# Ten projections' low weight parts: ACT negates the high part, a transfer issued by POOL adds the weight

## Chip, cores and metric

The kernel runs on one core of one Trainium2 chip. The metric is device time in microseconds. The engines are named as in the profile: PE (matrix products), PEld (its weight loads), DVE, ACT, POOL and SP (which issues most transfers).

## What is computed

One layer of a hybrid block on 512 tokens of width 1024. The change touches the first projection, `z = n1 @ w_in`, whose columns feed three consumers:

```python
n1 = rmsnorm(h, g_mix[i])
z = n1 @ w_in[i]
y_ssm = s5_mixer(z[..., OFF_SSM:OFF_Q], ...)                 # 512 columns
y_nsa = nsa_mixer(z[..., OFF_Q:OFF_KV], z[..., OFF_KV:OFF_NSA_GATE], z[..., OFF_NSA_GATE:OFF_MERGE], ...)
merge = jax.nn.sigmoid(z[..., OFF_MERGE:].astype(jnp.float32))
```

After it come the mix of both branches, an output product, a convolutional feed-forward part and a gated embedding.

## The kernel before

**Split products.** A product of two fp32 matrices is made of three products of a type with fewer bits. Each operand is split in a high part (a copy into that type, by ACT, L76) and a low part (operand minus high part, by DVE or POOL, L55); `mm3` (L83 to L85) multiplies high by high, high by low and low by high, all into one accumulator. The low-by-low product is left out.

**Projections.** `proj` computes 128 columns of `z` for all 512 tokens. It loads a 128x1024 tile of `w_in` (`wr`, 512 KB, `wraw`, L183), splits it into `wh` and `wl` (`wload`), and then runs `mm3` for each of KD = 8 slices: 24 products of 128x512. There are twelve calls: four for the SSM input (`un` copies, L590), four for the queries (`QT`), two for the compressed keys and values (`FL`) and two for the keys (`KK`). The first two get weights that were split earlier (`uw`); the other ten call `wload` with DVE as the engine for the low part. `wr` has three buffers, `wh` and `wl` two each, and the accumulators `pj` of the projections two (`acc`). A `wl` buffer is written again only when the projection two back has read it.

**Around them.** From the sixth projection on, PE does small products of the state-space part between them: `wbps` (transposes, L640), `wps` (L648), `tps` (L668), `yps` (L702, L705), four times over (`ssm_quarter`). Their operands come from all engines: `tab` (a table of rotations) and `x` (powers times an output matrix) from POOL, `z` and the scans from DVE, `Z`, `CX` and `WB` (copies) from ACT. The last of the ten projections is followed by the compression, the gates and attention.

**Order.** Each engine takes its instructions in one fixed order. In the first part (to the V columns) it is written by hand; in the part with the projections a planner sets it when the kernel is built, by its own table of costs. An instruction that waits holds up all behind it on its engine.

Of the kernel before, what the change touches and what calls it, by code (L numbers as in the profile page):

```python
# [9 lines left out]
F32 = mybir.dt.float32  # L10
F32R = mybir.dt.float32r
I32 = mybir.dt.int32
AF = mybir.ActivationFunctionType
# [3 lines left out]
MUL, ADD, SUB = ALU.mult, ALU.add, ALU.subtract  # L17

P = 128
# [3 lines left out]
KD = D // P  # L23
# [11 lines left out]
INW = 3864  # L35
# [10 lines left out]
def hybrid_kernel(ctx: ExitStack, tc: tile.TileContext, A, out):  # L46
    nc = tc.nc
    V, G, S, PE = nc.vector, nc.gpsimd, nc.scalar, nc.tensor

    def dr(name, off, ap):  # L50
        t = A[name]
        return bass.AP(tensor=t.tensor, offset=t.offset + off, ap=ap)
# [22 lines left out]
    def copy(o, a):  # L75
        S.activation(o, a, AF.Copy)  # L76

    def split(hi, lo, src, e=V):
        copy(hi, src)
        tt(lo, src, hi, SUB, e)  # L80

    def mm3(ps, lh, ll, rh, rl, start, stop):
        PE.matmul(ps, lh, rh, start=start, stop=False)  # L83
        PE.matmul(ps, lh, rl, start=False, stop=False)  # L84
        PE.matmul(ps, ll, rh, start=False, stop=stop)  # L85

    def pool(name, bufs=1, side=None, space=None):
        kw = {"name": name, "bufs": bufs, "reuse_waits": "tile"}
        if side:
            kw["side"] = side  # L90
        if space is not None:
            kw["space"] = space
        return tc.tile_pool(**kw)
# [3 lines left out]
    pw = ctx.enter_context(pool("weights", 2))  # L97
# [3 lines left out]
    def bank(tag, name):  # L101
        return psp.tile([P, 512], F32, tag=tag, name=name, bufs=BANKS[tag])

    def slot(p, tag, shape, dt, name):
        return p.tile(shape, dt, tag=tag, name=name, bufs=1)
# [69 lines left out]
    def either():  # L175
        turn[0] ^= 1
        return ("acc", "o")[turn[0]]

    def wraw(name, ld, row0, c0, kt, c, raw=None):
        if raw is None:  # L180
            raw = pw.tile([P, kt * c], F32, name="wr", tag="wr", bufs=3)
            raw = raw.rearrange("p (k c) -> p k c", k=kt)
        nc.sync.dma_start(raw, dr(name, row0 * ld + c0, [[ld, P], [P * ld, kt], [1, c]]))  # L183
        return raw

    def wload(name, ld, row0, c0, kt, c, e=V, keep=None, raw=None):
        if raw is None:
            raw = wraw(name, ld, row0, c0, kt, c)
        if keep is None:
            hi = pw.tile([P, kt * c], F32R, name="wh", tag="wh").rearrange("p (k c) -> p k c", k=kt)  # L190
            lo = pw.tile([P, kt * c], F32R, name="wl", tag="wl").rearrange("p (k c) -> p k c", k=kt)
        else:
            hi, lo = keep
        split(hi, lo, raw, e)
        return hi, lo

    def proj(c0, e=V, w=None):
        hi, lo = w or wload("w_in", INW, 0, c0, KD, P, e)
        ps = bank("acc", "pj")
        for k in range(KD):  # L200
            mm3(ps, hi[:, k], lo[:, k], n1h[:, k], n1l[:, k], k == 0, k == KD - 1)
        return ps

    n1h = slot(pn, "nh", [P, KD, T], F32R, "n1h")
    n1l = slot(pn, "nl", [P, KD, T], F32R, "n1l")
# [347 lines left out]
    for lv in range(5):  # L553
        n = 1 << lv
# [32 lines left out]
    for ct in range(4):  # L587
        un = pw.tile([P, L, NCH], F32, name="un", tag="mg")
        copy(un, proj(ct * P, w=uw[ct] if ct < 2 else None).rearrange("p (c j) -> p j c", j=L))
        nc.sync.dma_start(ud[ct], un)  # L590
        for j in range(L):
            n = L - 1 - j
            nc.sync.dma_start(Uc[32 * n:32 * n + 32, 4 * ct:4 * ct + 4], ud[ct, :, j].rearrange("(a c) k -> c a k", c=32))
# [135 lines left out]
    def compress_in(i):  # L729
        ps = proj(OFF_KV + i * P)  # L730
        for g in range(2):
            for j in range(2):
                x = ps[64 * g:64 * g + 64, j:j + 1]
                (V.tensor_copy if g else copy)(
                    FL[64 * j:64 * j + 64, i, :, g, 0:NCMP - 1],
                    bass.AP(tensor=x.tensor, offset=x.offset, ap=[x.ap[0], [2, 16], [16, NCMP - 1]]))

    def queries(i):
        ps = proj(OFF_Q + i * P)
        split(QT[:, i, 0], QT[:, i, 1], ps)  # L740
# [123 lines left out]
    for hc in range(2):  # L864
        hi, lo = wload("ssm_w_glu", SSMW, 0, hc * 256, 4, 256, V)
        if hc == 0:
            compressed_t(NQ - 1, scs[NQ - 1])
        for cc in range(2):
            c = 2 * hc + cc
            ps = bank(either(), "glu")  # L870
# [160 lines left out]
    for d2 in range(4):  # L1031
        hi, lo = wload("w_br_nsa", D, 0, d2 * 256, 4, 256, V)
        for dd in range(2):
            dt_ = 2 * d2 + dd
            ps = bank(either(), "br")
            for k in range(4):
                c = dd * P
# [22 lines left out]
    ps = bank("s", "cvps")  # L1060
# [8 lines left out]
    for qp in range(2):  # L1069
        for hf, qt in ((0, 0), (0, 1), (1, 0), (1, 1)) if qp == 0 else ((0, 2), (1, 2), (0, 3), (1, 3)):  # L1070
            cs = slice(hf * 512, hf * 512 + 512)
            qs_ = slice(qt * P, (qt + 1) * P)
            ps = bank(either(), "wo")
# [164 lines left out]
    with tc.manual_schedule(engines={mybir.EngineType.PE}):  # L1238
# [17 lines left out]
        for c in range(NR):  # L1256
            for i in range(2):
                hi, lo = wload("w_down", D, 2 * c * P, i * 512, 2, 512)
# [61 lines left out]
        for n, c in enumerate(range(NR, NP)):  # L1320
            h = hid[c]
            hi, lo = wload(None, 0, 0, 0, 2, 512, raw=b1[c].parts())
# [217 lines left out]
```

## Time and profile before

| | |
|---|---|
| time, median of 3 runs | 823.71 us (823.54 to 823.76) |
| the profiled execution | 823.98 us |
| its span in the trace | 822.2 us |
| PE busy | 803.7 us, 98% |
| DVE, ACT, POOL busy | 526.8, 395.4, 256.3 us |
| granted PE clock, mean | 0.997 of full speed |

The profile is one execution. Its own time is 1.8 us longer than its span, and 0.27 us above the median of the runs. Idle time of an engine costs something only where the engine is the one that sets the end. Matmuls overlap: one of 128x512 shows 0.39 us, while the next starts 0.23 us after it.

### The profile page before, as it was taken

How to read it: one execution, taken by the hardware profiler on the slowest of the kernel's cores; microseconds unless marked ns; L12 is line 12 of the kernel's file. 1: busy time of each engine (PE TensorE's matmuls, PEld its weight loads, DVE VectorE, ACT ScalarE, POOL GpSimd, SP SyncE). 2: the span in 40 equal slices, each digit the busy share in tenths (PEclk: the TensorE clock that was granted, in tenths of full speed). 3: DMA queues.
4: the chain of work that ended last, by engine and by line, in shares of the span. 5: the costliest groups of instructions: out<-in, count | busy, mean ns of one | idle time of the engine just before them, and what ended most of it. 6: DMA issues, size and time to landing. Idle time of an engine off the chain costs nothing. (4 is left out here: it accounts for less than half of the span.)

```text
span 822.2 us, 12258 instructions
## 1 busy us (share of the span) xinstructions
PE 803.7 (98%) x4523; PEld 674.4 (82%) x4523; DVE 526.8 (64%) x1102; ACT 395.4 (48%) x734; POOL 256.3 (31%) x316
## 2 busy tenths in 40 slices
PE   6999999999999999999999999999999999999995
PEld 5877889888888888888898888888888888888885
DVE  6899988757677631685444444554445759998743
ACT  4437553546777743434443444444434433675422
POOL 6595111126555633231033223333333100000411
PEclk9999999999999999999999999999999999999998
DMA  9663322423334323343052333323332453332011
GB/s 242 165 167 103 92 65 65 104 77 103 78 78 121 111 56 103 126 134 99 1 154 78 103 102 103 102 85 96 103 91 89 125 170 141 103 128 78 26 52 51
DMA packets 112001, 83.66 MB, mean 102 GB/s; under 512 B 9665, under 2 KB 97477, under 8 KB 111942
## 3 DMA queue, kind: packets, MB, share of 16 engines
q1 hardware_dynamic: 111262, 81.82, 34.5%
q10 hardware_dynamic: 680, 1.07, 0.3%
q8 instruction: 35, 0.57, 0.3%
q14 instruction: 24, 0.20, 0.1%
HBM read 75.54 MB, written 3.15 MB: 96 GB/s over the span
## 5 line engine op out<-in xcount | busy, mean ns | idle before, releaser
L55 POOL TENSOR_TENSOR wl<-wr,wh 128x1024 fp32r<-128x1024 f32 x39 | 94.0, 2409 | 247.8 <-ACT wh L76 229.9
L76 ACT ACTIVATE wh<-wr 128x1024 fp32r<-128x1024 f32 x88 | 93.1, 1059 | 93.7 <-issue 27.7
L55 DVE TENSOR_TENSOR wl<-wr,wh 128x1024 fp32r<-128x1024 f32 x49 | 62.7, 1280 | 54.0 <-ACT wh L76 54.0
L83 PE MATMUL pj<-n1h,wh 128*128 128x512 f32 x224 | 91.0, 406 | 0.3 <-ACT un L76 0.3
L85 PE MATMUL pj<-n1h,wl 128*128 128x512 f32 x224 | 88.1, 394 | 0.4 <-DVE wl L55 0.4
L84 PE MATMUL pj<-n1l,wh 128*128 128x512 f32 x224 | 88.0, 393 | 0.0
L64 DVE SCALAR_TENSOR_TENSOR cv<-ub,cvp,cv 128x511 f32<-128x511 f32 (+1 forms) x44 | 32.9, 748 | 66.2 <-ACT cv L1202 65.4
L84 PE MATMUL ua<-n2l,wh 128*128 128x512 f32 (+1 forms) x176 | 66.9, 380 | 0.2 <-DVE n2l L64 0.2
L83 PE MATMUL ua<-n2h,wh 128*128 128x512 f32 (+1 forms) x176 | 66.9, 380 | 0.0
L84 PE MATMUL ub<-n2l,wh 128*128 128x512 f32 (+1 forms) x176 | 66.8, 379 | 0.0
L85 PE MATMUL ua<-n2h,wl 128*128 128x512 f32 (+1 forms) x176 | 66.8, 379 | 0.0
L85 PE MATMUL ub<-n2h,wl 128*128 128x512 f32 (+1 forms) x176 | 66.8, 379 | 0.0
L83 PE MATMUL ub<-n2h,wh 128*128 128x512 f32 (+1 forms) x176 | 66.8, 379 | 0.0
L85 PEld LDWEIGHTS pj<-n1h,wl 128*128 128x128 f32 x224 | 42.1, 188 | 10.2 <-DVE wl L55 1.1
L61 POOL TENSOR_SCALAR pr<-pr,su,gates 128x512 f32<-128x512 f32 (+1 forms) x64 | 39.2, 623 | 31.1 <-DVE su L913 28.5
L83 PEld LDWEIGHTS pj<-n1h,wh 128*128 128x128 f32 x224 | 42.1, 188 | 8.0 <-ACT un L76 0.6
L84 PEld LDWEIGHTS pj<-n1l,wh 128*128 128x128 f32 x224 | 42.2, 188 | 7.7 <-issue 0.6
L55 POOL TENSOR_TENSOR wg1l<-wr,wg1h 128x1024 fp32r<-128x1024 f32 x2 | 7.0, 3506 | 111.1 <-ACT wg1h L76 111.1
L55 DVE TENSOR_TENSOR pl<-ptp,ph 128x128 fp32r<-128x128 f32 (+1 forms) x64 | 31.2, 488 | 15.2 <-ACT ph L76 14.9
L912 ACT ACTIVATE pr<-pr,nb 128x512 f32<-128x512 f32 (+1 forms) x64 | 35.6, 557 | 7.2 <-DVE nb L910 7.2
L76 ACT ACTIVATE ph<-ptp 128x128 fp32r<-128x128 f32 (+1 forms) x64 | 27.7, 433 | 22.9 <-PE ptp L921 22.4
L84 PEld LDWEIGHTS ua<-n2l,wh 128*128 128x128 f32 x176 | 33.1, 188 | 6.7 <-DVE n2l L64 0.4
(506 smaller groups left out, 2079.6 us busy)
## 6 DMA issues: line engine op xcount, KB each, us to landing
wr<-in_w_up_dram SPq DMA_DIRECT2D x44, 512.0 KB, 3.9
wr<-in_w_in_dram SPq DMA_DIRECT2D x28, 512.0 KB, 4.0
b<-in_w_down_dram SPq DMA_DIRECT2D x14, 512.0 KB, 3.5
QQ<-QT SPq DMA_DIRECT2D x16, 256.0 KB, 3.7
wr<-in_w_out_dram SPq DMA_DIRECT2D x8, 512.0 KB, 3.6
wr<-in_w_down_dram SPq DMA_DIRECT2D x8, 512.0 KB
wr<-in_w_ple_gate_dram SPq DMA_DIRECT2D x8, 512.0 KB, 3.4
xall<-in_x_dram SPq DMA_DIRECT2D x4, 512.0 KB
```

The costliest lines, as they stand in the source:

```text
L55: e.tensor_tensor(o, a, b, op=op)
L61: e.tensor_scalar(o, a, s1, s2, op0=op0, op1=op1)
L64: e.scalar_tensor_tensor(o, a, s, b, op0=op0, op1=op1)
L76: S.activation(o, a, AF.Copy)
L83: PE.matmul(ps, lh, rh, start=start, stop=False)
L84: PE.matmul(ps, lh, rl, start=False, stop=False)
L85: PE.matmul(ps, ll, rh, start=False, stop=stop)
L912: S.activation(pp, pp, AF.Exp, bias=nb, scale=-1.0, accum_out=su)
```

## The change

Ten of the twelve projections get their low part by another route. ACT copies the weight into `wh` as before. Then ACT writes minus `wh` into `wl`, and POOL issues a transfer that reads the same tile of `w_in` from memory again and adds it onto `wl`. The DVE subtraction is gone, and `wr` is read by the ACT copy alone. In all twelve projections the eight products with `wl` now come after the sixteen with `wh`.

```diff
+    def wload_added(c0):
+        raw = wraw("w_in", INW, 0, c0, KD, P)
+        hi, lo = (pw.tile([P, KD * P], F32R, name=n, tag=n).rearrange("p (k c) -> p k c", k=KD) for n in ("wh", "wl"))
+        copy(hi, raw)
+        S.activation(lo, hi.bitcast(F32), AF.Copy, scale=-1.0)
+        G.dma_start(lo, dr("w_in", c0, [[INW, P], [P * INW, KD], [1, P]]), accum_op=ADD)
+        return hi, lo
+
-    def proj(c0, e=V, w=None):
-        hi, lo = w or wload("w_in", INW, 0, c0, KD, P, e)
+    def proj(c0, w=None):
+        hi, lo = w or wload_added(c0)
         ps = bank("acc", "pj")
         for k in range(KD):
-            mm3(ps, hi[:, k], lo[:, k], n1h[:, k], n1l[:, k], k == 0, k == KD - 1)
+            PE.matmul(ps, hi[:, k], n1h[:, k], start=k == 0, stop=False)
+            PE.matmul(ps, hi[:, k], n1l[:, k], start=False, stop=False)
+        for k in range(KD):
+            PE.matmul(ps, lo[:, k], n1h[:, k], start=False, stop=k == KD - 1)
         return ps
```

The planner orders the engines anew from the third projection to the gates; from the scores of attention on the order is the same. The new instructions have line numbers up to 12 higher. The low parts of the third to the seventh projection are called `wl_725`, `wl_764`, `wl_840`, `wl_874` and `wl_1084` in the new program, the accumulators `pj_729`, `pj_768`, `pj_844`, `pj_878` and `pj_1088`.

PE at the end of the fifth projection and in the sixth, before (`pj_841` is the fifth, `pj_874` the sixth):

```order
L85 MATMUL pj_841<-n1h_74,wl_838 128x512
L640 MATMUL wbps_931<-ident_69,Z00_797 128x128 x2
L83 MATMUL pj_874<-n1h_74,wh_870 128x512
L84 MATMUL pj_874<-n1l_75,wh_870 128x512
L640 MATMUL wbps_931<-ident_69,Z00_797 128x128 x2
L85 MATMUL pj_874<-n1h_74,wl_871 128x512
```

And the same place of PE after the change (eleven products of the sixth projection stand ahead of the second row):

```order
L210 MATMUL pj_878<-n1h_74,wh_873 128x512
L213 MATMUL pj_844<-n1h_74,wl_840 128x512 x8
L211 MATMUL pj_878<-n1l_75,wh_873 128x512
L210 MATMUL pj_878<-n1h_74,wh_873 128x512
L211 MATMUL pj_878<-n1l_75,wh_873 128x512
L210 MATMUL pj_878<-n1h_74,wh_873 128x512
L211 MATMUL pj_878<-n1l_75,wh_873 128x512
L652 MATMUL wbps_935<-ident_69,Z00_799 128x128 x4
L652 MATMUL wbps_942<-ident_69,Z10_800 128x128 x4
L213 MATMUL pj_878<-n1h_74,wl_874 128x512 x8
```

The low products of the fifth projection have moved into the sixth, and those of the sixth behind both groups of transposes.

POOL between the last masks and the third set of `x`, before:

```order
L582 AFFINE_SELECT blk_652<-blk_652 128x4
L676 MEMSET dec_999 128x4
L55 TENSOR_TENSOR x0_917<-x0_917,x1_918 128x320
L583 AFFINE_SELECT blk_652<-blk_652 128x4
L55 TENSOR_TENSOR x1_925<-PI_89,CT_93 128x320
L55 TENSOR_TENSOR x0_924<-PR_88,CT_93 128x320
L55 TENSOR_TENSOR x0_924<-x0_924,x1_925 128x320
L55 TENSOR_TENSOR x1_1160<-PI_89,CT_93 128x320
L55 TENSOR_TENSOR x0_1159<-PR_88,CT_93 128x320
```

And after the change:

```order
L594 AFFINE_SELECT blk_652<-blk_652 128x4
L203 DMA wl_874<-in_w_in_dram 128x8x128
L688 MEMSET dec_1003 128x4
L55 TENSOR_TENSOR x0_921<-x0_921,x1_922 128x320
L595 AFFINE_SELECT blk_652<-blk_652 128x4
L55 TENSOR_TENSOR x1_929<-PI_89,CT_93 128x320
L55 TENSOR_TENSOR x0_928<-PR_88,CT_93 128x320
L55 TENSOR_TENSOR x0_928<-x0_928,x1_929 128x320
L55 TENSOR_TENSOR x1_1166<-PI_89,CT_93 128x320
L203 DMA wl_1084<-in_w_in_dram 128x8x128
L55 TENSOR_TENSOR x0_1165<-PR_88,CT_93 128x320
```

Two issues have come between the same operations. The three earlier ones (`wl_725`, `wl_764`, `wl_840`) stand ahead of the first operation on `tab`, ahead of the first 128x128 one, and ahead of the last one on `tab`; for the second of them the difference is this:

```order
 L55 TENSOR_TENSOR tab0_94<-tab0_94,tabm0_600 128x16x4
 L55 TENSOR_TENSOR tab1_95<-tab1_95,tabm1_601 128x16x4
+L203 DMA wl_764<-in_w_in_dram 128x8x128
 L55 TENSOR_TENSOR tab0_94<-tab0_94,COS_86 128x16x8
 L55 TENSOR_TENSOR tabm0_600<-tab1_95,SIN_87 128x16x8
```

The transfer is issued when POOL has come to it, and what follows waits until it is issued.

## Rows read from the trace of the kernel before

**Rows 1.** The page, part 1: busy time and share of the span by engine.

```profile
PE 803.7 (98%) x4523; PEld 674.4 (82%) x4523; DVE 526.8 (64%) x1102; ACT 395.4 (48%) x734; POOL 256.3 (31%) x316
```

**Rows 2.** Busy time by window: length, PE, PEld, DVE, ACT, POOL, clock, transfer share, GB/s.

```profile
60.00:70.00 10.00, 8.52 (x40) 6.44 (x39) 9.30 (x13) 8.51 (x17) 7.29 (x9) 1.00 0.51 130
```

**Rows 3.** What PE waited for up to 150 us: total us, times, longest.

```profile
PE wps L648 <- ACT WB L76: 0.9, 1, 0.9
PE pj L85 <- DVE wl L55: 0.4, 2, 0.2
PE pj L83 <- ACT un L76: 0.3, 1, 0.3
PE tps L668 <- ACT tps L664: 0.2, 1, 0.2
```

**Rows 4.** Timeline of PE: start us, duration us, instruction.

```profile
38.10 0.60 PE L526 MATMUL cps<-ident,craw 128*128 128x128 f32 x4
...
42.44 0.39 PE L83 MATMUL pj<-n1h,wh 128*128 128x512 f32 x1
...
45.16 0.39 PE L83 MATMUL pj<-n1h,wh 128*128 128x512 f32 x1
...
85.70 0.60 PE L640 MATMUL wbps<-ident,Z 128*128 128x128 f32 x4
86.06 0.48 PE L83 MATMUL pj<-n1h,wh 128*128 128x512 f32 x1
86.37 0.40 PE L84 MATMUL pj<-n1l,wh 128*128 128x512 f32 x1
...
92.08 1.06 PE L648 MATMUL wps<-Uc,WB 128*128 128x128 f32 x8
```

**Rows 5.** Timeline of ACT: `CT` copies, a high part, the copy of an accumulator.

```profile
38.74 0.77 ACT L529 ACTIVATE CT<-cps 64x256 f32<-64x256 f32 x2 [3.48 <-PE cps L526]
...
44.51 1.06 ACT L76 ACTIVATE wh<-wr 128x1024 fp32r<-128x1024 f32 x1 [1.10 <-PE pj L84]
45.47 0.58 ACT L76 ACTIVATE un<-pj 128x512 f32<-128x512 f32 x1
```

**Rows 6.** Timeline of DVE: two of the ten low parts.

```profile
40.63 1.23 DVE L55 TENSOR_TENSOR wl<-wr,wh 128x1024 fp32r<-128x1024 f32 x1 [0.79 <-ACT wh L76]
...
54.34 1.77 DVE L55 TENSOR_TENSOR wl<-wr,wh 128x1024 fp32r<-128x1024 f32 x1
```

**Rows 7.** Timeline of POOL: tables, masks and powers (in brackets idle before, releaser).

```profile
42.46 0.54 POOL L55 TENSOR_TENSOR tab<-tab,COS 128x16 f32<-128x16 f32 x2 [8.58 <-DVE COS L55]
...
45.91 1.53 POOL L55 TENSOR_TENSOR tabm<-tab,SIN 128x64 f32<-128x64 f32 x2
...
48.23 0.40 POOL L55 TENSOR_TENSOR tab<-tab,COS 128x128 f32<-128x128 f32 x1
...
51.29 1.20 POOL L55 TENSOR_TENSOR tabm<-tab,SIN 128x256 f32<-128x256 f32 x2
...
53.21 1.82 POOL L55 TENSOR_TENSOR tab<-tab,tabm 128x256 f32<-128x256 f32 x2
...
59.68 0.10 POOL L676 MEMSET dec<- 128x4 f32 x1
...
63.98 0.93 POOL L55 TENSOR_TENSOR x<-PR,CT 128x320 f32<-128x320 f32 x1 [2.21 <-ACT CX L76]
...
66.99 0.73 POOL L55 TENSOR_TENSOR x<-PR,CT 128x320 f32<-128x320 f32 x1 [0.19 <-ACT CX L76]
```

**Rows 8.** Transfers by line up to 140 us: count, KB each, median us from issue to landing.

```profile
wr<-in_w_in_dram SPq DMA_DIRECT2D x16, 512.0 KB, 4.0
...
wk<-in_cmp_wk_dram SPq DMA_DIRECT2D x2, 512.0 KB, 5.5
```

**Rows 9.** An issue of such a transfer on SP's queue, and POOL's subtraction of such a tile.

```profile
41.88 0.37 SPq L183 DMA_DIRECT2D wr<-in_w_in_dram  x1
...
L55 POOL TENSOR_TENSOR wl<-wr,wh 128x1024 fp32r<-128x1024 f32 x39 | 94.0, 2409 | 247.8 <-ACT wh L76 229.9
```

## The prediction

> **What bounds the kernel now.** Read the shares of the span first: PE is busy 98% of it [rows 1], so the end can only move by what PE waits or by what its products cost; no other engine's work counts unless PE waits for it. Then the waits of PE in the first 150 us: from the projections on there are four kinds, together 0.9 + 0.4 + 0.3 + 0.2 = 1.8 us [rows 3]. They lie in the stretch where the projections meet the state-space part; in its worst ten microseconds PE is busy 8.52, while DVE has 9.30 and ACT 8.51 [rows 2]. After that PE has no wait that this change touches. So all that the change can win by waits is 1.8 us, and what it makes PE wait anew is lost one for one: the order on PE is fixed, and nothing later has room to give it back.
>
> **What it removes.** Ten DVE subtractions of 1.23 to 1.77 us [rows 6]. PE waits for them 0.4 us in all [rows 3]; the other waits (WB, un, tps) are for ACT copies whose inputs came late from a crowded DVE. In the new order the two groups of transposes stand a whole projection ahead of `wps`, so I count the 0.9 and the other 0.5 us as gone too: -1.8. PE also returns to large products less often. A pair of large products starts 0.227 us apart (12 products in 45.16 - 42.44 = 2.72); four transposes take 0.36 us to the next start where 4 x 128 columns at that pace would take 0.23, and the product after them takes 0.31 [rows 4]. A split of the stream thus costs some 0.2 us, and the new order has 15 returns up to the gates instead of 19: -0.8.
>
> **What it adds on ACT.** Ten copies of a 128x1024 tile, 1.06 us each by the row of `wh` [rows 5], 10.6 us. They hide behind PE: two `wl` buffers leave 5.45 us (24 x 0.227) per projection, of which ACT uses a copy of 0.58, `wh` and now the negation. Without that cover PE would wait again for WB and `tps`, 1.1 us. On SP's queue `wr` comes free after the ACT copy, earlier than now, so its loads are not later.
>
> **What it adds on POOL and the transfers.** This decides. A negation can start only when the projection two back has read its buffer; then POOL must reach the issue, and the data must land before the low products. Call B the time that POOL spends on one issue, and A the time from the start of an issue to PE's first low product. The trace has neither. B lies between SP's issue, 0.37, and POOL's own pass over such a tile, 2.41 [rows 9]; no row is nearer to either, and I take the middle, 1.4. A lies between the plain load, 4.0 us, and twice that, 8.0, since the transfer reads the destination as well as the weight [rows 8]; I take the middle, 6, and add 1.0 because POOL takes that much longer to issue than SP: 7.0. Neither can be negative.
>
> PE's side, with no new wait: the second projection starts at 39.0 (38.10, four transposes 0.36, a return 0.08, two products) [rows 4] and ends at 44.45. The sixteen high products take 3.63 us, the eight low ones 1.82. First low products: third projection 48.1; fourth 53.55; fifth 53.55 + 1.82 + 3.63 + eleven products of the sixth (2.5) = 61.5; sixth 61.5 + 1.82 + five products (1.1) + eight transposes (0.8) = 65.2; seventh 65.2 + 1.82 + 3.63 + `wps` (1.1) = 71.8.
>
> POOL's side: `CT` ends at 39.5, the copy 0.58 and the negation 1.06 follow [rows 5], so the first issue is at 41.2, and the first operation on `tab` at 41.2 + B = 42.6, where it is now [rows 7]. From there I take POOL's own distances now, less 0.9 us for the pair at 45.91 (1.53 us, between 0.54 for 16 columns and 1.20 for 256: taken 0.63) and 0.6 us for the pair at 53.21 (1.82 against 1.20), both stretched while DVE ran a subtraction [rows 6, 7]. Issues: fourth at 41.2 + B + (48.23 - 42.46) - 0.9 = 46.1 + B = 47.5; fifth, ahead of the second operation of the pair at 53.21, 51.7 + 2B = 54.5; sixth, ahead of `dec` at 59.68, 56.9 + 3B = 61.1; seventh, ahead of the `x` at 66.99, less the 2.21 us of waiting in between: 62.0 + 4B = 67.6 [rows 7].
>
> What is left between issue and need: third 48.1 - 41.2 = 6.9; fourth 6.0; fifth 7.0; sixth 4.1; seventh 4.2. The fifth, sixth and seventh are ready earlier but stand behind POOL's tables, masks and powers. With A = 7.0 PE is 0.1 us late at the third, 1.0 at the fourth, 2.9 at the sixth and no more at the seventh (these are delays of PE's clock as a whole; a later one adds only what goes beyond). From the eighth on the small products between the projections leave over 8 us, so no more comes. New wait: +2.9. What stands behind an issue on POOL (the `x` that ACT copies into `CX`) is needed by `tps` only after the seventh's first low product, so it has no price of its own.
>
> **Sum.** 823.98 - 1.8 - 0.8 + 2.9 = 824.3 for the profiled execution, which is 0.27 above the median; so 824.0.
>
> **Bounds.** With B = 0.37 and A = 4.0 nothing is late: 2.6 us gained, 821.1 at the median. With B = 2.41 and A = 8.0 the seventh has 4.2 - 4 x 1.0 = 0.2 us left: 7.8 late, net +5.2, 828.9. The two loads that shared the engines with others landed after 5.5 us [rows 8]; twice that, 11.0, gives 10.8 - 2.6 = +8.2, 831.9.
>
> **The rivals.** *Hidden transfers.* If A stays below some 5 us and B near 1, all is landed in time and the kernel gains 1.8 to 2.6 us: 821.1 to 821.9. For it speak the 4.0 us of the plain load; against it that each transfer has two operands, and that the engines of the transfers are already 51% busy there [rows 2]. The Trainium skill, "DMA: Bandwidth & Descriptors", section "Anatomy of one DMA — SWDGE (gpsimd) path", fits a transfer issued by POOL as about 2.0 us plus its bytes at 436 GB/s, which would be an estimated 3.2 us for 512 KB; by it this rival holds and the sum would be 821.1. No run shows a POOL transfer yet, and its fit is below the 4.0 us that this trace has for SP.
>
> *POOL's queue becomes the bound.* Each issue shifts all that follows on POOL, so the seventh has lost 4B. The new wait is A - 4.2 + 4 (B - 1.4); from A + 4 (B - 1.4) = 8.5 on the kernel is slower by more than 1.65 us. B = 2.0 with A = 7.6 gives 7.6 - 4.2 + 2.4 = 5.8, net +3.2: 826.9. For it speaks that POOL is busy 7.29 of 10 us there with DVE at 9.30 [rows 2], and that the pair at 53.21 shows POOL stretched by DVE. The Trainium skill, "SBUF — State Buffer", section "Who interferes with whom", says that a DVE operation that takes both ports keeps POOL from writing a transfer's descriptors; that would lengthen B and A and lead to this rival. No row here shows it.
>
> *The waits don't close.* ACT has 10.6 us more to do, and PE may still wait for WB and `tps`: +1.1 on my sum, 825.1, still within 0.2%.
>
> **Chances.** 0.2% is 1.65 us, about what a measurement of this kernel can tell from no change. Forecast with the third rival, 822.1 to 825.3: 0.4. Hidden transfers far enough to gain more than that: 0.2. POOL's queue: 0.4, with the larger part below 830. So faster 0.2, same 0.4, slower 0.4; the range from 821.1 to 830.0 leaves out the far end of the second rival.
>
> **What would show it.** Right: PE's waits list has low products (L213) waiting for a transfer, about 3 us in all, at the fourth and the sixth projection, and no DVE `wl` or WB. POOL's distance from `rho` to the seventh's issue tells B; the distance from a POOL issue to the first L213 product that waited for it tells A. If no L213 product waits, the first rival holds; if the seventh waits most, POOL's queue does. The prediction is wrong if later stages change: their order is the same, and PE should be as busy there as now.

## The result, and the profile after

The changed kernel takes 830.48 us (median of 4 runs, 829.37 to 830.78). The kernel before, run beside it, takes 823.74 (823.54 to 824.34). The ratio is 1.0078, with a 95% interval of 1.0061 to 1.0096: slower by 6.7 us by the medians, and 0.5 us above the upper end of the forecast range. The profiled execution took 830.36 us, its span is 828.5. Two single executions, of 1697 us in experiment 6 and of 3372 us of the kernel before, where all others of the same kernel took about 823, are in no ratio.

The shares of the span, after, to be read beside [rows 1]:

```profile
PE 804.8 (97%) x4523; PEld 676.5 (82%) x4523; DVE 516.9 (62%) x1092; ACT 405.0 (49%) x744; POOL 268.0 (32%) x326
```

PE's busy time rose by only 1.1 us; the rest of the loss is idle time. What PE waited for up to 150 us, after (total us, times, longest), shows where:

```profile
PE pj L213 <- DMA wl<-in_w_in_dram: 7.2, 2, 5.3
```

The four waits of [rows 3] are all gone, and one kind has taken their place: low products that wait for a transfer issued by POOL. PE's timeline after has both waits, at the third and the sixth projection (in brackets the idle time before the instruction and what ended it):

```profile
50.10 2.11 PE L213 MATMUL pj<-n1h,wl 128*128 128x512 f32 x8 [1.87 <-DMA wl<-in_w_in_dram]
...
72.89 3.78 PE L213 MATMUL pj<-n1h,wl 128*128 128x512 f32 x8 [5.29 <-DMA wl<-in_w_in_dram]
76.47 0.63 PE L210 MATMUL pj<-n1h,wh 128*128 128x512 f32 x1
76.89 0.55 PE L211 MATMUL pj<-n1l,wh 128*128 128x512 f32 x1
77.28 0.39 PE L210 MATMUL pj<-n1h,wh 128*128 128x512 f32 x1
```

The eight products after the second wait take 3.58 us to the next start (76.47 - 72.89); eight at the pace of [rows 4] take 1.82. The windows say why (length, busy time of PE, PEld, DVE, ACT, POOL, then PE's clock, the share of the transfer engines, GB/s):

```profile
68.00:70.00 2.00, 0.00 (x0) 0.00 (x0) 1.90 (x5) 1.95 (x5) 1.07 (x1) 1.00 1.29 202
70.00:72.00 2.00, 0.00 (x0) 0.00 (x0) 0.71 (x2) 1.98 (x4) 1.92 (x3) 0.60 1.24 256
72.00:74.00 2.00, 1.11 (x3) 0.92 (x4) 0.00 (x0) 0.39 (x1) 0.99 (x2) 0.50 1.39 186
74.00:76.00 2.00, 2.00 (x6) 1.56 (x5) 0.00 (x0) 0.00 (x0) 0.00 (x0) 0.50 1.35 215
76.00:78.00 2.00, 2.00 (x8) 1.57 (x7) 0.66 (x1) 1.29 (x2) 0.00 (x0) 0.69 0.71 184
```

While PE stood idle the granted clock fell from 1.00 to 0.50, that is from 2.4 to 1.2 GHz, and it came back only after PE had worked again for some 4 us. The price is read from the timeline: 3.58 - 1.82 = 1.76 us for the eight products and 0.42 + 0.39 - 0.45 = 0.36 for the next two starts, 2.1 us in all. The share of the transfer engines (overlapping packets count twice, so it can pass 1) is above 1.2 in each of these windows up to 76 us; in the whole stretch from 60 to 70 us it is 1.16, where [rows 2] has 0.51.

The transfers: first POOL's issues of the third to the seventh, with what POOL does between them left out. Then, of all ten, the length of an issue in ns and the time from its start to the landing in us, each as shortest/median/longest. Then the queue of POOL's transfers (packets, MB, share of all sixteen transfer engines) and the loads by SP, both up to 140 us:

```profile
41.36 1.77 POOL L203 DMA_DIRECT2D wl<-in_w_in_dram  x1 [7.80 <-ACT tab L570]
...
47.68 1.58 POOL L203 DMA_DIRECT2D wl<-in_w_in_dram  x1
...
55.22 1.94 POOL L203 DMA_DIRECT2D wl<-in_w_in_dram  x1
...
60.49 2.44 POOL L203 DMA_DIRECT2D wl<-in_w_in_dram  x1
...
68.93 1.58 POOL L203 DMA_DIRECT2D wl<-in_w_in_dram  x1 [1.28 <-ACT wl L202]
...
L203 POOL DMA_DIRECT2D wl<-in_w_in_dram x10: 1552/1575/2435, 41.4 to 113.5; - x10
DMA to landing us min/median/max: 6.4/7.4/12.4
```

```profile
q0 software_dynamic: 10400, 5.24, 31.1%
...
wr<-in_w_in_dram SPq DMA_DIRECT2D x16, 512.0 KB, 9.7
```

The third lands 50.10 - 41.36 = 8.7 us after the start of its issue, the sixth 72.89 - 60.49 = 12.4. The queue of POOL's transfers (q0) takes 31.1% of all sixteen engines over 140 us: 4.35 us of all sixteen for each transfer of 512 KB. SP's loads of the same size, 4.0 us in [rows 8], now land after 9.7.

**The account of the 6.3 us** between the spans (828.5 - 822.2): waits 7.2 more and 1.8 less, +5.4; the low clock, +2.1; fewer returns to large products, -0.8; sum +6.7, 0.4 more than the spans differ. From 80 us on PE has no wait in either kernel up to the gates, and its order is the same after them.

### The profile page after: what moved, and what is told of

The parts are those of the page before. It is cut to its first block, busy times and chain, and to the rows that moved or that the text cites. A ratio compares the mean times of both kernels' runs of the same rounds, so it can differ in the third digit from the quotient of the medians.

```text
span 828.5 us, 12288 instructions
## 1 busy us (share of the span) xinstructions
PE 804.8 (97%) x4523; PEld 676.5 (82%) x4523; DVE 516.9 (62%) x1092; ACT 405.0 (49%) x744; POOL 268.0 (32%) x326
## 5 line engine op out<-in xcount | busy, mean ns | idle before, releaser
L55 DVE TENSOR_TENSOR wl<-wr,wh 128x1024 fp32r<-128x1024 f32 x39 | 49.2, 1261 | 53.7 <-ACT wh L76 53.7
L83 PE MATMUL pj<-n1h,wh 128*128 128x512 f32 x128 | 52.9, 413 | 0.0
L84 PE MATMUL pj<-n1l,wh 128*128 128x512 f32 x128 | 50.2, 392 | 0.0
L85 PE MATMUL pj<-n1h,wl 128*128 128x512 f32 x128 | 49.9, 391 | 0.0
L55 DVE TENSOR_TENSOR pl<-ptp,ph 128x128 fp32r<-128x128 f32 (+1 forms) x64 | 31.1, 488 | 15.5 <-ACT ph L76 14.9
L85 PEld LDWEIGHTS ub<-n2h,wl 128*128 128x128 f32 x176 | 33.1, 188 | 6.3
L84 PEld LDWEIGHTS ub<-n2l,wh 128*128 128x128 f32 x176 | 33.0, 188 | 6.3
L85 PEld LDWEIGHTS ua<-n2h,wl 128*128 128x128 f32 x176 | 33.1, 188 | 6.2
```

Of the source, the lines that this page charges most:

```text
L55: e.tensor_tensor(o, a, b, op=op)
```

## Experiments

Each kernel is the changed one but for the lines shown. The planner orders each of them anew; where that matters it is said. Runs that were sent together share their runs of the kernel before, whose median lay between 823.81 and 823.97 us.

**1. The new order alone.** DVE makes the low parts as before; only the order of the products is new.

```diff
-        hi, lo = w or wload_added(c0)
+        hi, lo = w or wload("w_in", INW, 0, c0, KD, P, V)
```

> The low products come last in all twelve projections, as in the changed kernel, but DVE makes the low parts by its subtraction as in the kernel before: no negation, no transfer. Theory 1 (the whole loss comes from the transfers): no L213 product waits for more than 0.5 us, the 1.8 us of waits of the kernel before are partly gone, PE saves up to 0.8 us by fewer returns to large products; time 821.0 to 823.5, below the kernel before. Rival (the new order on PE itself costs, by the accumulators being held longer or by a lower granted clock): 825 or more.

Measured: 822.61 us (822.31 to 825.23, 11 runs), ratio to the kernel before 0.9984 (0.9975 to 0.9993). PE's waits in the stretch, and its share of the span:

```profile
PE pj L210 <- DVE QT L55: 1.2, 1, 1.2
PE wps L660 <- ACT WB L76: 0.2, 1, 0.2
...
PE 802.9 (98%) x4523; PEld 675.0 (82%) x4523; DVE 528.2 (64%) x1102; ACT 395.5 (48%) x734; POOL 259.3 (32%) x316
```

So the new order is worth 1.4 us, and it wins as forecast: PE has 0.8 us less to do (802.9 against 803.7), and of the old waits 0.2 us is left, though a wait of 1.2 us for DVE has come up (`QT`, the low part of an accumulator). The rest of the change then costs 830.48 - 822.61 = 7.9 us.

**2. The order and the negation, without the transfer.** DVE's subtraction overwrites what ACT has negated.

```diff
-        G.dma_start(lo, dr("w_in", c0, [[INW, P], [P * INW, KD], [1, P]]), accum_op=ADD)
+        tt(lo, raw, hi, SUB)
```

> As order_only, and ACT makes the negation too, which the DVE subtraction then overwrites: the price of ACT's 10.6 us alone. Theory 1 (the negation hides behind PE): time within 1 us of order_only, 821.8 to 823.8. Rival (the longer way over ACT makes PE wait, for WB, QT or the low parts): 824.5 or more.

Measured: 823.64 us (823.39 to 824.86, 10 runs), 1.0 us above experiment 1. PE waits 1.2 us for `QT`, as there, and for nothing of ACT; the 1.0 us is found in PE's busy time, 804.0 us against 802.9. PE's order differs in places between the two, so whether it is the negation's or the order's is open. It is small either way: 822.6 to 823.6 with no transfer, 830.5 with them.

**3. The same transfers without the addition.** All engines have word for word the order of the changed kernel.

```diff
-        G.dma_start(lo, dr("w_in", c0, [[INW, P], [P * INW, KD], [1, P]]), accum_op=ADD)
+        G.dma_start(lo, dr("w_in", c0, [[INW, P], [P * INW, KD], [1, P]]))
```

> The ten transfers that POOL issues write the weight over wl in place of adding it: the addition is left out, so the low parts are wrong. Every engine has the same instructions in the same order as the changed kernel. Theory 1 (the addition doubles what a transfer asks of the 16 transfer engines, 4.35 us of all sixteen per transfer, and these are full from 45 to 76 us): the share of the POOL queue falls to about half, the transfers land after 4 to 7 us, the third projection's wait of 1.87 us goes and the sixth's of 5.29 falls below 1.5; time 821.5 to 825. Theory 2 (a transfer issued by POOL is slow whatever it does, because of its own start or because it moves 1024 runs of 512 bytes): landing stays at 6.4 us or more in quiet stretches, the waits at the third and the sixth stay within 1 us of 1.9 and 5.3, time 829 to 831.

> The same kernel as the one with plain transfers, once more: its executions went from 820.7 to 827.3 us, and its one profile showed a fast one. If waits for transfers of varying length and the lower clock after them make the difference, a profile above 825 us shows an L213 wait of 1.5 us or more and a stretch of granted clock near 0.5; a profile near 821 shows neither.

Measured: 825.63 us (820.65 to 827.34, 10 runs) and, in a second set of runs, 824.35 (823.58 to 825.50, 8 runs). The first lies 0.6 above theory 1's range, and neither comes near theory 2's. The executions of this kernel differ more among themselves than those of the others; the two profiles are of executions of 821.41 and 823.58 us. In each, the only wait for a transfer is the one at the sixth projection. The first profile, then the second:

```profile
65.99 2.11 PE L213 MATMUL pj<-n1h,wl 128*128 128x512 f32 x8 [0.56 <-DMA wl<-in_w_in_dram]
...
L203 POOL DMA_DIRECT2D wl<-in_w_in_dram x10: 873/942/1139, 41.3 to 104.5; - x10
DMA to landing us min/median/max: 4.4/5.8/6.4
...
q0 software_dynamic: 10400, 5.24, 24.3%
```

```profile
68.18 2.11 PE L213 MATMUL pj<-n1h,wl 128*128 128x512 f32 x8 [2.68 <-DMA wl<-in_w_in_dram]
...
DMA to landing us min/median/max: 4.3/4.9/8.4
...
q0 software_dynamic: 10400, 5.24, 22.3%
```

So the addition is a cause: without it, in the same order, the issue takes POOL 0.94 us and not 1.57, the third does not wait, and the sixth lands after 6.4 and 8.4 us, not 12.4. But theory 1 had the size wrong: the queue's share fell from 31.1% to 24.3 and 22.3% (3.4 and 3.1 us of all sixteen engines per transfer), not to half, and in the second profile the sixth's wait is 2.68 us, not below 1.5. The 2.2 us between the profiled executions (821.41 and 823.58) are the 2.1 us between the waits, at a clock of 1.00 in both. So what the transfers meet on the engines differs from execution to execution, by 2 us of landing: while the sixth's transfer was under way, SP's queue moved 0.98 MB in the first profile and 1.69 in the second. No profile shows an execution above 825 us; their mean clock is lower (0.992 to 0.996), which is as far as the runs tell.

**4. An eighth of the data.**

```diff
-        G.dma_start(lo, dr("w_in", c0, [[INW, P], [P * INW, KD], [1, P]]), accum_op=ADD)
+        G.dma_start(lo[:, 0], dr("w_in", c0, [[INW, P], [1, P]]), accum_op=ADD)
```

> The ten transfers add one slice of eight only (64 KB in place of 512 KB); seven eighths of the addition are left out. As many issues at the same places of POOL's queue. Theory 1 (the data moved is what takes long): no product waits for a transfer, landing 2 to 4 us, time 821 to 822.5. Rival (POOL's queue: what stands behind an issue comes late because it is there at all, or the transfer has a fixed latency of more than 6.5 us): the sixth still waits for more than 3 us, time above 826.

Measured: 825.99 us (823.85 to 826.60, 10 runs), a miss in its time for theory 1. The profiled execution, 826.60 us, is the slowest of the ten; four took less than 825. Landing takes 2.6/2.7/5.4 us, an issue 0.88, and no product waits for a transfer, as theory 1 had it. But the planner had put the second half of `wbps`, `wps` and `tps` elsewhere, and PE waits there for ACT and DVE, and loses the clock again:

```profile
68.59 0.50 PE L210 MATMUL pj<-n1h,wh 128*128 128x512 f32 x1 [1.28 <-DVE QT L55]
...
75.38 1.32 PE L660 MATMUL wps<-Uc,WB 128*128 128x128 f32 x8 [1.83 <-ACT WB L76]
...
76.00:78.00 2.00, 2.00 (x39) 1.78 (x42) 1.26 (x3) 0.85 (x2) 1.75 (x3) 0.56 0.35 41
78.00:80.00 2.00, 2.00 (x25) 1.53 (x22) 1.23 (x3) 0.62 (x3) 1.68 (x3) 0.59 0.00 0
```

It shows that ten issues by POOL of 0.88 us each delay no low product; its time can't be compared.

**5. Long rows in place of short ones.** The 512 KB are read in 128 runs of 4 KB, not 1024 of 512 bytes: once from memory (the same 4 KB per partition for every projection, so the right values are left out), once from `wr` in SBUF (the right ones).

```diff
-        G.dma_start(lo, dr("w_in", c0, [[INW, P], [P * INW, KD], [1, P]]), accum_op=ADD)
+        G.dma_start(lo.rearrange("p k c -> p (k c)"), dr("w_in", 0, [[INW, P], [1, KD * P]]), accum_op=ADD)
```

> The transfers of POOL add 512 KB again, but the same contiguous rows of the weight for every projection (128 runs of 4 KB in place of 1024 of 512 bytes): what is added is not the tile's own weight, so the addition of the right values is left out. Theory A (the many 512-byte runs make the transfer slow and its issue long): an issue takes POOL about 0.9 us as with one slice, landing 4 us or less when quiet, the third does not wait, the sixth less than 1 us; time 821 to 825. Theory B (an addition is slow by its bytes): landing stays at 6 us and more, waits of 1 us and more at the third, sixth or seventh; time 826 to 831.

```diff
-        G.dma_start(lo, dr("w_in", c0, [[INW, P], [P * INW, KD], [1, P]]), accum_op=ADD)
+        G.dma_start(lo.rearrange("p k c -> p (k c)"), raw.rearrange("p k c -> p (k c)"), accum_op=ADD)
```

> The transfer of POOL adds the weight from its copy in SBUF (wr) instead of from memory: the same sum, 128 rows of 4 KB on both sides; wr stays taken until the transfer has landed. Theory A (the 512-byte runs): issue about 0.9 us, landing 4 us or less, waits below 1 us, time 821 to 825. Theory B (an addition is slow by its bytes, wherever they come from): landing 6 us and more, time 826 to 832. Either way the loads of wr start later by the time that the transfer takes.

Measured: 824.08 us (823.43 to 825.88, 10 runs) from memory; 823.25 us (822.53 to 824.34, 11 runs) from SBUF, ratio to the kernel before 0.9993 (0.9984 to 1.0002). From memory, then from SBUF:

```profile
PE pj L213 <- DMA wl<-in_w_in_dram: 1.2, 2, 0.9
...
L203 POOL DMA_DIRECT2D wl<-in_w_in_dram x10: 858/882/1207, 42.3 to 106.4; - x10
DMA to landing us min/median/max: 5.6/6.3/7.5
```

```profile
PE pj L213 <- DMA wl<-wr: 2.0, 2, 1.6
...
L203 POOL DMA_DIRECT2D wl<-wr x10: 854/880/1511, 40.9 to 105.8; - x10
DMA to landing us min/median/max: 4.6/5.8/8.1
```

With long rows the issue takes 0.88 us, no transfer lands after more than 8.1, PE waits 1.2 to 2.0 us in place of 7.2, and the loss against the kernel before is gone (0.6 to 1.5 us are left against experiment 1). Theory A is right in the times and the issue, and wrong in the landing, and from SBUF one wait, 1.6, is above its 1 us: a landing of 4 us or less was never reached with 512 KB, so an addition has a price by its bytes too. How much of the gain the rows make by themselves isn't separated. The planner ordered these kernels anew (POOL's first four issues stand within 2.3 us of those of the changed kernel), and while the sixth's transfer was under way SP's queue moved 0.56 MB (from memory) and 0.81 (from SBUF), where it moved 2.06 in the changed kernel (experiment 7 has that row). The shortest landings, of transfers with next to nothing beside them, compare better: 6.4 us in the change, 5.6 with long rows from memory, 4.6 from SBUF.

**6. Transfers only from the seventh projection on**, first as in the change, then from SBUF as in experiment 5.

```diff
+        count[0] += 1
-        hi, lo = w or wload_added(c0)
+        hi, lo = w or (wload_added(c0) if count[0] > 6 else wload("w_in", INW, 0, c0, KD, P, V))
```

> Low products last everywhere; the third to the sixth projection get their low parts by DVE, the last six by ACT's negation and the transfer. Theory 1 (the transfers hurt only where the transfer engines are full, up to 76 us, and where little lies between issue and need): no wait for a transfer above 0.5 us, time 821 to 823.5. Rival (every transfer costs through the loads that it delays or through POOL): waits of 1 us and more at the seventh or later, time 825 or more.

> As the one that makes the first four low parts by DVE and transfers only from the seventh projection on, but the transfer adds the weight from its copy in SBUF (wr), 128 rows of 4 KB. If the long rows are what counts: landing 4 to 5 us in place of 6.5 to 7.4, the seventh's wait falls from 2.7 us to 0 to 1, time 821.5 to 823.5, about that of the kernel with the new order alone (822.6). If not: 2 to 3 us of wait, 825 to 827.

> The same kernel as the one that transfers from SBUF from the seventh projection on, for its profile: its one profiled execution took twice as long as all others and says nothing. Its time was 822.75 us, 2.7 to 3.6 below that of its twin with transfers from memory. If the long rows are the reason, the six transfers land after 4 to 5 us (6.5 to 7.4 in the twin), an issue takes POOL about 0.9 us (1.57), and the wait of 2.7 us at the seventh is 1 us or less.

Measured: 826.37 us (824.49 to 828.09, 11 runs) from memory; from SBUF 822.75 (median of 12 runs; ratio 0.9985, 0.9975 to 0.9994) and, in a second set of runs, whose profile is shown, 822.83 (822.72 to 823.66, 8 runs; ratio 0.9989, 0.9978 to 1.0001). From memory, then from SBUF:

```profile
L203 POOL DMA_DIRECT2D wl<-in_w_in_dram x6: 1542/1568/1780, 67.9 to 107.5; - x6
DMA to landing us min/median/max: 6.5/6.8/7.4
...
74.54 2.11 PE L216 MATMUL pj<-n1h,wl 128*128 128x512 f32 x8 [2.70 <-DMA wl<-in_w_in_dram]
```

```profile
L203 POOL DMA_DIRECT2D wl<-wr x6: 852/880/1089, 67.8 to 105.6; - x6
DMA to landing us min/median/max: 4.5/4.8/6.2
...
72.61 2.08 PE L216 MATMUL pj<-n1h,wl 128*128 128x512 f32 x8 [0.99 <-DMA wl<-wr]
```

The first of the pair is a miss for theory 1, and its rival, 825 us or more with a wait at the seventh, came true: with the four earlier transfers gone, one of the change still takes 6.5 us and more. Most of that is its own price: the last of the ten in the changed kernel, with 0.02 MB of SP's beside it (the last row of the second fence of experiment 7), lands after 6.4. PE waits 2.7 us for the first of the six, issued at 67.92 for a need at 71.84. Long rows from SBUF, the two together, cut the landing by 2.0 us in the median and the wait by 1.7. In these profiles the six later ones delay nothing but this one product. But the profile from memory is of an execution of 824.94 us, the second shortest of the eleven; most took 826.3 to 826.7 at a lower mean clock, and no profile shows one of those.

**7. One transfer only, at the sixth projection** (`count[0] == 6` in the line of experiment 6).

> Low products last everywhere; only the sixth projection gets its low part by the negation and the transfer, the others by DVE. Theory 1 (the 12.4 us of the sixth come from competition: its own earlier transfers and the loads that these hold up): the one transfer lands after 6.4 to 7.5 us, and PE waits for it by 0 to 3 us, according to how long before its need it is issued. Rival (the sixth is slow by itself, because of what else moves there, Uc and un): landing 10 us or more, wait 4 us or more.

Measured: 828.85 us (828.71 to 829.11, 4 runs).

```profile
62.20 1.78 POOL L203 DMA_DIRECT2D wl<-in_w_in_dram  x1 [1.05 <-ACT wl L202]
...
DMA to landing us min/median/max: 7.9/7.9/7.9
...
70.14 3.78 PE L216 MATMUL pj<-n1h,wl 128*128 128x512 f32 x8 [4.59 <-DMA wl<-in_w_in_dram]
```

What the engines moved from the issue to the landing (queue, packets, MB, share; q1 is SP's): the sixth in the changed kernel, the sixth here, and the last of the ten in the changed kernel:

```profile
q1 hardware_dynamic: 3440, 2.06, 67.1%
q0 software_dynamic: 1548, 0.78, 50.3%
...
q1 hardware_dynamic: 751, 0.39, 21.7%
...
q1 hardware_dynamic: 34, 0.02, 2.8%
```

This divides the sixth's 12.4 us: 6.4 in quiet, 7.9 with 0.39 MB of SP's transfers beside it, and the other 4.5 in the company of the changed kernel, of which SP's queue has 2.06 MB and POOL's other transfers only 0.26 (0.78 - 0.52). That POOL's earlier transfers are what bunched SP's loads there fits their landing (4.0 us before, 9.7 after), but no run shows it by itself. Each theory had a part: the landing is 0.4 us above theory 1's range, and the wait of 4.6 us is the rival's. The issue comes at 62.20 here, 1.7 us later than in the changed kernel, for a need at 65.55. One transfer of ten, with a wait of 4.6 us and the low clock after it, costs 6.2 us against experiment 1.

**8. Work for PE during the wait.** Twenty products into a bank that nobody reads; the two groups of transposes now come after the sixth's low products.

```diff
+        if count[0] == 6:
+            fp = bank("o", "fp")
+            for k in range(20):
+                PE.matmul(fp, hi[:, k % KD], n1h[:, k % KD], start=k == 0, stop=k == 19)
         for k in range(KD):
             PE.matmul(ps, lo[:, k], n1h[:, k], start=False, stop=k == KD - 1)
```

> The changed kernel with 20 more products of 128x512 (4.5 us at full clock) on PE around the sixth projection's place, into a bank that nobody reads: six of them within its high products, fourteen ahead of its low products; the two groups of transposes come after the low products here. The transfers are as in the changed kernel. Theory 4 (in the changed kernel 5.3 us of idle PE also lower its clock, for 2.1 us more): the idle time at the sixth falls to about 1 us, the clock stays at 1.00 from 60 to 80 us, and the time falls by about 2 us, to 827 to 829, though PE has 4.5 us more to do. Rival (the clock has nothing to do with it; PE loses only what it waits): the extra work takes the place of the wait, time 830 to 831.5.

Measured: 828.71 us (827.85 to 829.00, 4 runs), 1.8 us less than the changed kernel though PE has 20 x 0.227 = 4.5 us more to do.

```profile
72.59 2.12 PE L220 MATMUL pj<-n1h,wl 128*128 128x512 f32 x8 [1.33 <-DMA wl<-in_w_in_dram]
...
70.00:72.00 2.00, 1.26 (x6) 0.72 (x4) 0.67 (x2) 0.31 (x1) 1.92 (x3) 1.00 1.24 253
72.00:74.00 2.00, 1.41 (x6) 1.19 (x7) 0.00 (x0) 1.70 (x3) 1.67 (x3) 1.00 1.38 201
```

The transfer is as late as before (72.59 - 60.45 = 12.1 us), the clock stays at 1.00, and the account closes: 4.5 us of work added, 4.0 us of idle time removed (5.29 - 1.33), 2.1 us of low clock saved, together -1.6; the spans differ by 827.1 - 828.5 = -1.4. So the clock's part of the loss is shown.

## Why the prediction was wrong

**The step that failed is A, the time from an issue to the first low product.** It was taken as one figure, 7.0 us, in the middle of 4.0 and 8.0, from a plain load that SP issues into a half idle stretch. It measured 8.7 at the third projection and 12.4 at the sixth, and the new waits came to 7.2 us where 2.9 were forecast. Two things were missed. In quiet the transfer itself takes 6.4, at 4.35 us of all sixteen engines each; without the addition these are 4.3 us and 3.1 to 3.4 (experiment 3). And five of them are issued within 28 us (41.36 to 68.93): 5 x 4.35 = 21.8 us of all engines in little more than that, beside SP's loads. A grows with the company, which one figure for all five can't show (experiment 7: 7.9 with 0.39 MB of SP's beside it, 12.4 with 2.06 MB of SP's and 0.26 of POOL's). That SP's loads would not be later fell with it: they landed after 9.7 us in the median and not 4.0. The row of loads that shared the engines, 5.5 against 4.0 [rows 8], stood in the prediction, and its double, 11.0, gave 831.9 us; I left that end out of the range.

**A term that was missing: the clock.** A new idle time was priced one for one. The wait of 5.3 us cost 2.1 more after it. With A as measured and no clock the prediction's own sum is 823.71 - 1.8 - 0.8 + 7.2 = 828.3, within the range; with 2.1 it is 830.4, against 830.48 measured. Without that term the miss of A alone would have stayed inside.

**What held.** PE's needs: the third 48.23 (50.10 - 1.87; forecast 48.1), the sixth 67.60, or 65.73 without the earlier delay (65.2). POOL's issues: 41.36, 47.68, 55.22, 60.49 (41.2, 47.5, 54.5, 61.1); the seventh, at 68.93 (67.6), waited 1.28 us for its negation, which ACT began at 67.58, behind copies of which one had waited for DVE. B: 1.57 us in the median (1.4), though, where POOL's next operation follows at once, it shows a start 0.9 to 1.2 us after that of the issue. The four waits gone, -1.8: all gone. Fewer returns, -0.8: experiment 1 has just that in PE's busy time, though experiment 2, with much the same order, does not (804.0). ACT's negation, 10.6 us, made PE wait nowhere in the changed kernel. Later stages: unchanged. The fourth was forecast 1.0 us late in all and was not, since the third's 1.87 us of delay had given it more time; the fifth and the seventh did not wait.

**The rivals.** *Hidden transfers* fell: no transfer of the change landed in under 6.4 us. The fit of the Trainium skill, "DMA: Bandwidth & Descriptors", section "Anatomy of one DMA — SWDGE (gpsimd) path", would be an estimated 3.2 us for 512 KB; the trace doesn't agree here: 4.3 us is the shortest without the addition, 6.4 with it, and the measurement decides. *POOL's queue* fell as a mechanism though its time, 826.9, was on the right side: issues grew up to 2.44 us (what lengthened them is open; without the addition, in the same order, none took more than 1.14), but the sixth's came 0.6 us earlier than forecast and its products waited for data, and the seventh's did not wait. *The waits don't close* fell too: no wait for WB or `tps` is left.

## What to carry to other kernels

A transfer that is to replace an engine's work must be priced at its own time in the crowd that it makes: count what each takes of all engines (here 4.35 us), add the loads that overlap, and compare the sum with the stretch, before the latency of a single one is laid against a need. Look at the rows it moves and at where else the data already lies: the same sum, read from SBUF in rows of 4 KB, cost 0.88 us of POOL per issue in place of 1.57, and 7 us less in all (in an order that the planner had changed too). And price a new idle time of PE with what its clock does afterwards. Of the versions tried, the new order of the products with DVE's subtraction (822.61 us) and the same with the last six additions read from SBUF (822.75) beat both kernels, the one before by 0.1 to 0.2%, which the second set of the latter leaves open (its interval reaches 1.0001); the two can't be told apart.

## What was not expected of the hardware

- An issue by POOL has a length of its own: 0.88 us for 128 rows with an addition, 0.94 for 1024 rows without one, 1.57 (up to 2.44) for 1024 rows with one, all as medians. Neither rows nor addition alone lengthens it much.
- Of all sixteen engines, 512 KB took 4.35 us with the addition and short rows, 3.40 and 3.12 without the addition (24.3 and 22.3% of 140 us for ten), 3.18 with long rows from memory (22.7%), 2.87 with long rows from SBUF (20.5%).
- SP's loads pay as well: 4.0 to 9.7 us in the changed kernel. That cost PE nothing here: it waits for no `wh`.
- The share of the engines is no measure of lateness by itself: from 60 to 70 us it was 1.31 without the addition (first profile), at 278 GB/s, and 1.16 with it, at 226 GB/s; the addition moves less in the same time.
- The granted clock stayed at 1.00 through waits of 2.7 us (experiments 3 and 6) and fell to 0.50 in waits of 4.6 and 5.3. In experiment 4 it fell after two waits of 1.3 and 1.8 us; why there and not after the longer single ones, no run here settles.
